# Gate products made early in place of plain gate units, in a hybrid retention and attention block

## The chip, the cores and the metric

The kernel runs on one core of one Trainium2 chip. The metric is the time of one execution in microseconds (us) on the device; the time shown for a kernel is the median of its runs. The engines are TensorE (PE, matmuls, with PEld for its weight loads), VectorE (DVE), ScalarE (ACT), GpSimd (POOL) and SyncE (SP, which issues most DMAs).

## What is computed

The input has 1024 tokens of 1024 channels; 16 meta tokens stand ahead of them. One input projection of the normalised tokens feeds everything else:

```python
u = rms_norm(h)
rq, rk, rv, rg, aq, ak, av, ag, gr, ga = split(u @ w_in)
o_r = groupnorm(retention_forward(rq, rk, rv) + retention_backward(rq, rk, rv))  # 4 heads, chunks of 128
y_r = (o_r * silu(rg)) @ w_rb
o_a = window_attention(aq, ak, av, sink)        # 8 heads, window of +-128, meta keys, sink
y_a = (o_a * silu(ag)) @ w_ab
out = (sigmoid(gr) * y_r + sigmoid(ga) * y_a) @ w_out
return h + rms_norm(out)
```

The gate columns of `w_in` are `rg`, `ag`, `gr` and `ga`: 4096 columns, 16 **units** of 256 columns.

## The kernel before

**Precision.** All matmuls that matter are made three times, for the float32 result: each operand is split into a high part (a copy in the matmul's format) and a low part (what the copy lost), and `mm3` (lines 69 to 71) adds high x high, low x high and high x low into the same PSUM bank. So one product of two 128-wide blocks is three matmuls, and every operand costs a copy (ACT or POOL) and a subtraction on DVE (`dve_lo`, line 77).

**Order of the work.** The code writes the program in one order; a scheduler then keeps that order as priorities and, on each engine, may take a later instruction when an earlier one is not ready. Tiles with the same tag share a fixed number of buffers, and `tc.issue_after(x)` puts what follows behind `x` on x's engine. The stages are:

1. Setup, and the first retention head's queries and keys.
2. Retention, heads 0 to 3 (`retention`). Each head has a forward pass over 9 chunks (`stage1` projects the values with `projT`, transposes the keys and makes scores; `stage2` makes the chunk's output `pa` and the state product `pkv`) and a backward pass over the chunks (`pb`, the normalisation, and the transposes `to` in `finish`). In the backward pass `fill(KT)` asks seven times for eight **fill steps**: pieces of an independent projection, each of three matmuls (one `mm3`), that PE does while the chain over the chunks waits. For heads 0 to 2 the filler is the next head's queries and keys (`gen_qk`). For head 3 it is the attention's keys, its first queries and one plain gate unit, `gen_gate(7)`. What the fills have not used, `drain()` does at the end of the head.
3. Attention, in four pairs of heads (`attention`), 8 blocks of 128 queries each. `FILL` says how many fill steps follow each block. For the last pair the filler is the second half of its queries (16 steps) and the plain gate units 6 and 5.
4. The phases z, r, a and o (`Phase` and `run`): the gate units, the two branch projections and the output projection. They use a seven-product form of the 2x2 block product: the weight unit is cut into 2x2 blocks A11 to A22, the input into B11 to B22, and seven products of 12 matmuls (4 x `mm3`, 512 columns) replace eight.

**A plain gate unit** (`gen_gate`, line 701) makes a gate unit in the ordinary way: 4 tiles of 8 x 3 matmuls, 96 in all, one fill step per `mm3`; DVE scales each tile, ACT takes the tanh and SP stores it. `N_GATE = 3` units are made so, and the other 13 run in phase z.

**A unit in z** goes through products 1, 5, 6, 2, 7, 3, 4, and two units are interleaved (u, u+1 at each product). `prepare` makes the left operand (sums of weight blocks into `st` tiles, then `split` into `lh` and `ll`), `LEAD = 6` jobs ahead: the step of product i prepares job i+5. `product` runs the 12 matmuls into a PSUM bank, `combine` adds the banks up:

- Products 1, 6, 7 and 4 add into one bank, X. After product 1 ACT copies it (`c1`), after 6 again (`u2`), after 7 again (`u3`); each copy has to be made before the next product adds to X.
- Product 2 goes to a bank Z, and `c1 + Z` is the output block (0, 0). Products 5 and 3 go to Y: `u3 + Y` after product 5 is block (1, 1), and `u2 + Y` after product 3 is block (0, 1). X after product 4 is block (1, 0).
- `z_post` scales a block (line 1006), takes SiLU or tanh, and for the first 8 units multiplies it by the branch output `v`, fetched from DRAM (`z_fetch`, tiles `g`).

When the last products of z have used the input blocks, `refill` loads the next phase's input and makes its blocks and differences: 28 splits (`split_b`, ACT copy at line 752 and `dve_lo`) and 16 subtractions (line 924). `refill` returns a table: at step -13 before the end of the phase do this, at -11 that. In between, `pre_split` makes the blocks of `w_out` for phase o at steps 30, 40, 50 and 60.

**Buffers named below.** `pj`: three PSUM banks for projections and fill steps. `wr`: two raw weight tiles; `wh` and `wl`: four split halves of a unit each. `g`: six tiles of 512 columns, shared by `v` and others.

Of the kernel before, what the change touches and what calls it, by code (L numbers as in the profile page):

```python
# [38 lines left out]
def block_kernel(ctx: ExitStack, tc: tile.TileContext, xT, x, w_in, w_rb, w_ab, w_out, vecs, dec, sink,  # L39
# [20 lines left out]
    mx_d = dram.tile([KT, P, SEQ], F32, tag="mx", name="mx_d")  # L60
    tg_d = dram.tile([2 * KT, P, SEQ], F32, tag="tg", name="tg_d")

    xs_d = {n: dram.tile([4, P, 512], F32, tag=f"xs{n}", name=f"xs{n}") for n in ("T1", "T2", "T3", "T4")}
    pre_d = {n: [dram.tile([P, 4, 512], F32, tag=f"pre{n}{s}", name=f"pre{n}{s}") for s in range(2)]
             for n in ("T1", "T2", "T3", "T4")}
# [363 lines left out]

    pend = []  # L430

    def retention(h, fill):
        q, kt = qk[h]
        qh, ql = [], []
        for i in range(2):
# [62 lines left out]
        def stage2(c):  # L498
            n, vh, vl, kd, s = st1.pop(c)
            if c > 0:  # L500
                fh, fl = state["fs"]
                pa = p3(f"pa{h}_{c}")
                mm3(pa[:, 0:256], s[0], s[1], vh, vl, True, True)
                mm3(pa[:, 256:512], qs(qh, c), qs(ql, c), fh, fl, True, True)
                o = op[c - 1]
                nc.scalar.activation(o, pa[:, 0:256], AF.Copy, scale=rcol[:, c:c + 1])
                nc.vector.scalar_tensor_tensor(o, pa[:, 256:512], qdf(h, c), o, op0=ALU.mult, op1=ALU.add)
            if kd:
                pk = p2(f"pkv{h}_{c}")
            if "f" in kd:  # L510
                a, b = kd["f"]
                mm3(pk[:, 0:256], a[0:n], b[0:n], vh[0:n], vl[0:n], True, True)
                new = rp.tile([P, 256], F32, tag="S", bufs=2, name=f"Sf{h}_{c}")
                if c == 0:
                    nc.vector.tensor_copy(new, pk[:, 0:256])
                else:
                    nc.vector.scalar_tensor_tensor(new, state["f"], cdf(h), pk[:, 0:256], op0=ALU.mult, op1=ALU.add)
                state["f"] = new
                state["fs"] = split_state(new, f"f{h}_{c}")
            if "b" in kd:  # L520
                a, b = kd["b"]
                mm3(pk[:, 256:512], a, b, vh, vl, True, True)
                nc.scalar.copy(kvb[c - 1], pk[:, 256:512])
# [174 lines left out]
            dve_lo(l, x[o], h)  # L698
            nc.sync.dma_start(pre_d[n][1][:, k], l.bitcast(F32))

    def gen_gate(u):

        w = load_w(w_in, U_GR + u)
        for a, b in HALVES:
            for e_ in range(2):
                t = yield from proj(w, P * e_, a, b, f"pgt{u}_{a}{e_}")
                o = ra.tile([P, 512], F32, tag="m1", bufs=2, name=f"gt{u}_{a}{e_}")
                nc.vector.tensor_tensor(o, t, rbc[:, a:b], ALU.mult)
                nc.scalar.activation(o, o, AF.Tanh, scale=0.5)
                nc.sync.dma_start(tg_d[2 * u + e_, :, a - NM:b - NM], o)  # L710
                yield

    with tc.issue_after(normed):
        evac_qk0(2)
        decay_table((0,))
        evac_qk0(3, 5)
    for h in range(NH):
        fill, drain = filler([*([gen_qk(h + 1)] if h < 3 else [gen_ak(0), gen_aq(0, 0), gen_gate(7)])])
        if h == 0:
            with tc.issue_after(normed):  # L720
                nc.vector.tensor_tensor(qd, rcol[:, 1:9].unsqueeze(1).to_broadcast([P, 2 * NH, NB]),
                                        dtab[:, 8:16].unsqueeze(2).to_broadcast([P, 2 * NH, NB]), ALU.mult)
        with tc.issue_after(rotated):
            retention(h, fill)
            drain()
    while pend:
        pend.pop(0)()
# [25 lines left out]
        dve_lo(l[:, k], src, h[:, k])  # L753

    class Phase:
        def __init__(self, nm, seq, load, post, fetch=None, apart=(), early=()):
            self.nm, self.seq, self.load, self.post, self.fetch = nm, seq, load, post, fetch
            self.apart, self.early = apart, early
            self.raw, self.s, self.ops, self.u = {}, {}, {}, {}
            self.cur = None  # L760

        def block(self, u, n):
# [16 lines left out]
        def prepare(self, u, p):  # L779
            if self.cur is not None and u // 2 != self.cur:  # L780
                self.raw = {}
            self.cur = u // 2
            g = nc.vector.tensor_tensor
            if self.fetch and p in POST and u not in self.early:
                self.fetch(u, *POST[p])
            if p in (1, 2, 4):
                self.split(u, p, self.block(u, PROD[p][0]))
            elif p == 7:
                t = lp.tile([P, 4, P], F32, tag="st", bufs=3, name=f"st{self.nm}{u}S3")
                g(t, self.block(u, "A11"), self.block(u, "A21"), sub)  # L790
                self.split(u, 7, t)
            elif p == 5:
                t = self.s[u] = lp.tile([P, 4, P], F32, tag="st", bufs=3, name=f"st{self.nm}{u}S")
                g(t, self.block(u, "A21"), self.block(u, "A22"), add)
                self.split(u, 5, t)
                g(t, t, self.block(u, "A11"), sub)
            elif p == 6:
                t = self.s[u]
                self.split(u, 6, t)
                if u in self.early:  # L800
# [43 lines left out]
        def combine(self, u, p, st):  # L844
# [42 lines left out]
            if "u3" in st and "Y" in st and "c22" not in st:  # L887
                st["c22"] = plus(new("c5") if (self.nm, u) == last[:2] else st["u3"], st["u3"], "Y")
                self.post(u, 1, 1, st["c22"])
                if early:  # L890
                    done("Y")

    LEAD = 6
# [18 lines left out]
    def refill(nm, src):  # L912
# [199 lines left out]
    def o_tail(o, a):  # L1112
# [4 lines left out]
        if a:  # L1117
# [6 lines left out]
    gates = [U_G + u for u in range(4)] + [U_AG + u for u in range(4)] + [U_GR + u for u in range(8)]  # L1124
# [175 lines left out]
    def fills(hp):  # L1300
# [127 lines left out]
```

## Time and profile before

| what | value |
|---|---|
| median of 3 runs | 1092.71 us (1090.38 to 1093.98) |
| the profiled execution | 1091.82 us |
| its span, first to last instruction | 1089.8 us |
| mean granted PE clock | 0.995 |
| data moved by DMA | 159.45 MB, 146 GB/s on average |

The profile is one execution. Its span leaves out what lies before the first and after the last instruction, here 2.0 us. "Busy" is the time in which an engine executes; matmuls overlap in the pipeline, so PE's busy time says only that it has work. In a row of stretches "(x904)" is the number of instructions that touch the stretch, and the last columns are the granted clock of PE as a share of full speed, the DMA engines' share and GB/s. In a row of groups, the numbers behind the bar are busy us, mean ns of one, and then the engine's idle time before them with who ended it. The names are those of the program's tiles: `bz` is a bank of phase z, `pgt` one of a plain gate unit.

### The profile page before, as it was taken

The numbers are of one execution on the slowest core, as the hardware profiler recorded it, in microseconds if no ns is written. First come the engines' busy times: TensorE is split into PE (matmuls) and PEld (weight loads), VectorE is DVE, ScalarE is ACT, GpSimd is POOL, SyncE is SP. The second block draws the span as 40 slices with busy tenths as digits, with TensorE's granted clock in tenths as the row PEclk, the third lists the DMA queues.
The fourth block names the chain that finished last, engine by engine and source line by source line (L and its number), as shares of the span: only waits on it lengthen the run. The fifth ranks groups of instructions, "written<-read, shape, count | busy, mean of one in ns | idle before, by whom it ended". The sixth has DMA issues, their size and how long they took to land.

```text
span 1089.8 us, 17221 instructions
## 1 busy us (share of the span) xinstructions
PE 1068.6 (98%) x5975; PEld 922.5 (85%) x5975; DVE 872.3 (80%) x1864; ACT 488.6 (45%) x1132; POOL 241.7 (22%) x346
## 2 busy tenths in 40 slices
PE   8999999999999999999999999999999999999996
PEld 7899999998989889988887888888888788787885
DVE  7897778877955988898667975888889899767765
ACT  7241432513314544545657643454456546433442
POOL 3235324233322544445220000000000000110032
PEclk9999999998999999999999999999999999999999
DMA  7121101111114871112115663779874755779463
GB/s 289 39 79 40 55 24 59 59 40 39 63 44 144 295 277 60 59 59 68 50 49 169 238 227 120 247 240 324 276 274 140 236 185 200 235 202 336 118 116 78
DMA packets 75799, 159.45 MB, mean 146 GB/s; under 512 B 8128, under 2 KB 19904, under 8 KB 74944
## 3 DMA queue, kind: packets, MB, share of 16 engines
q1 hardware_dynamic: 71824, 151.78, 40.4%
q0 software_dynamic: 3456, 6.29, 3.7%
q8 instruction: 47, 0.77, 0.3%
q10 hardware_dynamic: 432, 0.28, 0.1%
q14 instruction: 40, 0.33, 0.1%
HBM read 105.89 MB, written 52.43 MB: 145 GB/s over the span
## 4 chain that ended last, share of the span: by engine, by line
PE 86%; DVE 5%; issue 3%; DMA 3%; POOL 2%; ACT 1%; SPq 0%; POOLq 0%; DVEq 0%; ACTq 0%
PE bz L70 8%; PE bz L69 8%; PE bz L71 8%; PE pv L69 3%; PE pv L70 3%; PE pv L71 3%; PE br L70 2%; PE bo L70 2%; PE bo L69 2%; PE bo L71 2%; PE br L69 2%; PE br L71 2%; PE ba L70 2%; PE ba L71 2%; PE ba L69 2%
## 5 line engine op out<-in xcount | busy, mean ns | idle before, releaser
L1054 POOL DMA_DIRECT2D mx_d<-c1a x4 | 3.7, 918 | 391.5 <-DVE c1a L1045 391.5
L70 PE MATMUL bz<-big,llz 128*128 128x512 f32 x208 | 82.4, 396 | 0.0
L71 PE MATMUL bz<-big,lhz 128*128 128x512 f32 x208 | 81.9, 394 | 0.0
L69 PE MATMUL bz<-big,lhz 128*128 128x512 f32 x208 | 80.8, 394 | 0.0
L69 PE MATMUL pv<-wh,big 128*128 128x256 f32 x256 | 73.6, 288 | 1.3 <-DVE m_qk L162 1.3
L70 PE MATMUL pv<-wh,big 128*128 128x256 f32 x256 | 73.4, 287 | 0.0
L71 PE MATMUL pv<-wl,big 128*128 128x256 f32 x256 | 73.2, 286 | 0.0
L69 PE MATMUL bz<-T,lhz 128*128 128x512 f32 x156 | 61.6, 395 | 0.0
L70 PE MATMUL bz<-T,llz 128*128 128x512 f32 x156 | 61.5, 395 | 0.0
L71 PE MATMUL bz<-T,lhz 128*128 128x512 f32 x156 | 61.3, 394 | 0.0
L1205 ACT ACTIVATE p<-p,nm 128x400 f32<-128x400 f32 (+1 forms) x64 | 38.3, 598 | 44.0 <-DVE nm L1203 42.3
L77 DVE TENSOR_TENSOR wl<-wr,wh 128x1024 fp32r<-128x1024 f32 x34 | 47.4, 1398 | 4.6 <-POOL wh L74 4.4
L70 PE MATMUL paq<-big,wl 128*128 128x512 f32 x128 | 51.0, 398 | 0.0
L71 PE MATMUL paq<-big,wh 128*128 128x512 f32 x128 | 50.9, 398 | 0.0
L69 PE MATMUL paq<-big,wh 128*128 128x512 f32 x128 | 50.8, 397 | 0.1
L69 PEld LDWEIGHTS pv<-wh,big 128*128 128x128 f32 x256 | 48.9, 191 | 2.1 <-DVE m_qk L162 1.5
L1217 POOL TENSOR_SCALAR p<-p,den 128x400 f32<-128x400 f32 (+1 forms) x60 | 36.0, 610 | 63.9 <-DVE den L1211 52.0
L70 PEld LDWEIGHTS pv<-wh,big 128*128 128x128 f32 x256 | 48.9, 191 | 0.1
L71 PEld LDWEIGHTS pv<-wl,big 128*128 128x128 f32 x256 | 48.9, 191 | 0.0
L69 PEld LDWEIGHTS bz<-big,lhz 128*128 128x128 f32 x208 | 39.0, 188 | 9.4
L70 PEld LDWEIGHTS bz<-big,llz 128*128 128x128 f32 x208 | 39.1, 188 | 9.3 <-DVE llz L77 0.2
L71 PEld LDWEIGHTS bz<-big,lhz 128*128 128x128 f32 x208 | 39.2, 188 | 8.9
(616 smaller groups left out, 3641.0 us busy)
## 6 DMA issues: line engine op xcount, KB each, us to landing
wr<-in_w_in_dram SPq DMA_DIRECT2D x35, 512.0 KB, 3.6
wrz<-in_w_in_dram SPq DMA_DIRECT2D x28, 512.0 KB, 5.7
tg<-tg_d SPq DMA_DIRECT2D x32, 256.0 KB, 4.7
T<-preT SPq DMA_DIRECT2D x6, 1024.0 KB, 7.5
oTr_d<-ost SPq DMA_DIRECT2D x16, 256.0 KB, 2.1
xs<-in_xT_dram SPq DMA_DIRECT2D x16, 256.0 KB, 5.5
xsT<-xs SPq DMA_DIRECT2D x16, 256.0 KB, 5.7
oTa_d<-oa SPq DMA_DIRECT2D x16, 256.0 KB, 2.1
```

The source lines that it names most:

```text
L69: nc.tensor.matmul(o, ah, bh, start=first, stop=False, **kw)
L70: nc.tensor.matmul(o, al, bh, start=False, stop=False, **kw)
L71: return nc.tensor.matmul(o, ah, bl, start=False, stop=last, **kw).ins
L77: return nc.vector.tensor_tensor(o, i, hi.bitcast(F32), ALU.subtract).ins
L1054: nc.gpsimd.dma_start(d, to, accum_op=ALU.add)
L1205: nc.scalar.activation(p[:, 0:wid], p[:, 0:wid], AF.Exp, scale=-1.0, bias=nm_[:, e_:e_ + 1], accum_out=den[:, e_:e_ + 1])
L1217: nc.gpsimd.tensor_scalar(pt[e_][:, 0:wid], pt[e_][:, 0:wid], den[:, e_:e_ + 1], 1.0, op0=ALU.mult, op1=ALU.mult)
```

## The change

The plain gate units go (`N_GATE`, `gen_gate`), and all 16 gate units run in phase z. In their place 22 of the units' products are made early and kept in DRAM: product 2 for units 2 to 15, and product 3 also for units 8 to 15 (`PRE`). `gen_pre` loads the raw weights, makes the left operand (for a unit with two products with three DVE sums over 512 columns), splits it, runs 4 fill steps per product into a `pj` bank, copies the bank with ACT and stores it in `e_d`.

These fill steps stand at three places. In heads 1, 2 and 3 of the retention `between` asks, behind the forward state product of chunks 0 to 3, for one step (heads 1 and 2) or two (head 3). In the backward pass of head 3 a piece of 16 steps takes the place of the 32 steps of `gen_gate(7)`, between the keys and the queries. In the last attention pair the remaining 56 steps take the place of the 64 of `gen_gate(6)` and `gen_gate(5)`.

In z, `Phase` leaves the made products out of its sequence. Product 1's step fetches `e` for product 2 into a `g` tile and adds it to `c1`; product 6's step fetches `e` for product 3, and `u2` becomes the DVE sum of `e` and bank X where it was ACT's copy of X. The order of a unit is so 1, 5, 6, 7, 3, 4 for units 2 to 7 and 1, 5, 6, 7, 4 for units 8 to 15. The refill at the end of z has a table of its own.

```diff
-FILL = {**{h: (8, 8, 0, 8, 8, 8, 8, 0) for h in range(3)}, 3: (16, 16, 0, 16, 14, 10, 8, 0)}
-N_GATE = 3
+FILL = {**{h: (8, 8, 0, 8, 8, 8, 8, 0) for h in range(3)}, 3: (16, 16, 0, 14, 10, 8, 8, 0)}
+PRE = {u: (2, 3) if u > 7 else (2,) for u in range(2, 16)}
...
-                mm3(pk[:, 0:256], a[0:n], b[0:n], vh[0:n], vl[0:n], True, True)
+                forward = mm3(pk[:, 0:256], a[0:n], b[0:n], vh[0:n], vl[0:n], True, True)
+                if h and c < 4:
+                    with tc.issue_after(forward):
+                        between(h // 3 + 1)
...
+    def gen_pre(u):
+        g = nc.vector.tensor_tensor
+        n = P * len(PRE[u])
+        raw = [keep.tile([P, 4, 256], F32, tag="wr", bufs=2, name=f"we{u}_{j}") for j in range(len(PRE[u]))]
+        for j, t in enumerate(reversed(raw)):
+            nc.sync.dma_start(t[:, :, 0:n], w_in[gates[u], :, 4 - 4 * j:8 - 4 * j, 0:n])
+        t = raw[-1]
+        if n > P:
+            v = t[:, :, P:n]
+            g(v, raw[0][:, :, P:n], v, ALU.add)
+            g(v, v, raw[0][:, :, 0:P], ALU.subtract)
+            g(v, t[:, :, 0:P], v, ALU.subtract)
+        h = wp.tile([P, 4, 256], R, tag="wh", bufs=4, name=f"weh{u}")[:, :, 0:n]
+        l = wp.tile([P, 4, 256], R, tag="wl", bufs=4, name=f"wel{u}")[:, :, 0:n]
+        nc.scalar.copy(h, t[:, :, 0:n])
+        dve_lo(l, t[:, :, 0:n], h)
+        for p in PRE[u]:
+            b = pj(f"pe{u}_{p}")
+            m = slice(P * (p - 2), P * (p - 1))
+            c = slice(NM + 512 * (p - 2), NM + 512 * (p - 1))
+            for k in range(4):
+                mm3(b, h[:, k, m], l[:, k, m], xh[4 + k][:, c], xl[4 + k][:, c], k == 0, k == 3, True)
+                if k < 3:
+                    yield
+            o = ra.tile([P, 512], F32, tag=f"m{p - 1}", bufs=2, name=f"e{u}_{p}")
+            nc.scalar.copy(o, b)
+            nc.sync.dma_start(e_d[u, p], o)
+            yield
...
-        fill, drain = filler([*([gen_qk(h + 1)] if h < 3 else [gen_ak(0), gen_aq(0, 0), gen_gate(7)])])
+        fill, drain = filler([*([gen_qk(h + 1)] if h < 3 else [gen_ak(0), pieces(pre, 16), gen_aq(0, 0)])])
...
-            retention(h, fill)
+            retention(h, fill, filler([pieces(pre, (0, 4, 4, 8)[h])])[0])
...
             if p == 1:
                 copy("c1")
+                e = self.e.pop((u, 2), None)
+                if e is not None:
+                    nc.vector.tensor_tensor(st["c1"], st["c1"], e, add)
+                    self.post(u, 0, 0, st["c1"])
+            elif p == 6 and (u, 3) in self.e:
+                st["u2"] = new("u2")
+                plus(st["u2"], self.e.pop((u, 3)), "X")
+                self.post(u, 0, 1, plus(st["u2"], st["u2"], "Y"))
...
+        if nm == "z":
+            return {-16: [load(0, 0), load(0, 1)], -13: [load(1, 1)], -11: [plain("B22", 1, 1)],
+                    -9: [plain("B11", 0, 0)], -7: [t1, load(1, 0)], -5: [t2, t3], -4: [b21], -3: [plain("T3", 0, 1)],
+                    -1: [plain("T4", 0, 0)]}
...
-    steps = run([(Phase("z", sequence(16 - N_GATE, (1, 3, 2, 5, 6, 7, 4)), w_loader(w_in, gates), z_post, z_fetch,
-                        early=(0, 1)),
+    steps = run([(Phase("z", sequence(16, (1, 3, 2, 5, 6, 7, 4)), w_loader(w_in, gates), z_post, z_fetch,
+                        early=(0, 1), pre=PRE),
...
-            l += [gen_gate(6), gen_gate(5)]
+            l.append(pre)
```

Before, the table that z used was the common one: the splits of B11 at -13, `t1` at -11, `t2` and `t3` at -9, `b21` at -7, T3 at -5, B22 at -3 and T4 at -1.

More of the change, by code (lines that the diff above doesn't have):

```diff
@@ L430, in block_kernel, with retention @@
     pend = []
-    def retention(h, fill):
+    def retention(h, fill, between):
         q, kt = qk[h]
@@ L699, in pre_split, with pieces, all_pre @@
             nc.sync.dma_start(pre_d[n][1][:, k], l.bitcast(F32))
[L701 to L711, printed above, removed]
+    gates = [U_G + u for u in range(4)] + [U_AG + u for u in range(4)] + [U_GR + u for u in range(8)]
+    def gen_pre(u):
[26 more added lines that the diff above has]
+            yield
+    def pieces(gen, n):
+        for _ in range(n):
+            yield next(gen)
+    def all_pre():
+        for u in PRE:
+            yield from gen_pre(u)
+    pre = all_pre()
     with tc.issue_after(normed):
@@ L755, in block_kernel, with __init__ @@
     class Phase:
-        def __init__(self, nm, seq, load, post, fetch=None, apart=(), early=()):
-            self.nm, self.seq, self.load, self.post, self.fetch = nm, seq, load, post, fetch
+        def __init__(self, nm, seq, load, post, fetch=None, apart=(), early=(), pre={}):
+            self.nm, self.load, self.post, self.fetch, self.pre = nm, load, post, fetch, pre
+            self.seq = [(u, p) for u, p in seq if p not in pre.get(u, ())]
             self.apart, self.early = apart, early
-            self.raw, self.s, self.ops, self.u = {}, {}, {}, {}
+            self.raw, self.s, self.ops, self.u, self.e = {}, {}, {}, {}, {}
             self.cur = None
@@ L783, in prepare @@
             g = nc.vector.tensor_tensor
-            if self.fetch and p in POST and u not in self.early:
-                self.fetch(u, *POST[p])
+            made = {1: 2, 6: 3}.get(p)
+            if made not in self.pre.get(u, ()):
+                made = None
+            for q in (p, made):
+                if self.fetch and q in POST and u not in self.early:
+                    self.fetch(u, *POST[q])
+            if made:
+                self.e[u, made] = gtile(f"e{u}{made}")
+                nc.sync.dma_start(self.e[u, made], e_d[u, made])
             if p in (1, 2, 4):
@@ L799, in prepare @@
                 self.split(u, 6, t)
-                if u in self.early:
+                if u in self.early or 3 in self.pre.get(u, ()):
                     del self.s[u]
@@ L889, in combine @@
                 self.post(u, 1, 1, st["c22"])
-                if early:
+                if early or 3 in self.pre.get(u, ()):
                     done("Y")
```

2 lines of the change are left out of this document (1 added, 1 removed).

## The prediction

> **What bounds the kernel now.** I read the page first, then busy time by stretch, the groups of matmuls, and TensorE's (PE's) own waits.
>
> ```profile
> span 1089.8 us, 17221 instructions
> PE 1068.6 (98%) x5975; PEld 922.5 (85%) x5975; DVE 872.3 (80%) x1864; ACT 488.6 (45%) x1132; POOL 241.7 (22%) x346
> PE 86%; DVE 5%; issue 3%; DMA 3%; POOL 2%; ACT 1%; SPq 0%; POOLq 0%; DVEq 0%; ACTq 0%
> ```
>
> PE is busy for 98% of the span and carries 86% of the chain that ended last; VectorE (DVE) is second with 80%. The next rows are stretches of time, with busy us and instruction count of PE, PEld, DVE, ACT and POOL, then the granted PE clock and the DMA share. The first three are the borders between retention heads, then attention, its last head pair, the gate phase z, and the stretch in which z turns into the next phase, r.
>
> ```profile
> 118.00:126.00 8.00, 7.38 (x57) 6.50 (x56) 6.16 (x21) 3.77 (x12) 2.87 (x5) 1.00 0.14 45
> 186.00:194.00 8.00, 7.37 (x57) 6.50 (x56) 6.13 (x21) 3.77 (x12) 2.48 (x5) 1.00 0.19 63
> 254.00:268.00 14.00, 12.09 (x70) 10.79 (x69) 10.46 (x33) 4.97 (x17) 3.86 (x7) 0.76 0.12 39
> 340.00:500.00 160.00, 159.10 (x968) 141.25 (x967) 135.02 (x330) 77.72 (x228) 72.67 (x107) 1.00 0.41 142
> 500.00:588.00 88.00, 87.08 (x512) 76.34 (x510) 58.82 (x183) 53.42 (x156) 24.80 (x50) 1.00 0.20 70
> 590.00:798.00 208.00, 208.00 (x904) 168.47 (x903) 171.90 (x280) 106.33 (x190) 0.00 (x0) 1.00 0.71 244
> 798.00:858.00 60.00, 60.00 (x258) 48.14 (x257) 58.69 (x98) 38.16 (x69) 0.00 (x0) 1.00 0.60 201
> ```
>
> In z PE never rests. One matmul lasts 394 ns in the rows below, but they overlap: 904 touch the 208 us stretch, so one starts every (208 + 0.39) / 904 = 0.2305 us. That pitch, not the duration, is the price of a 512-column matmul. So a **product** (12 matmuls) is 2.77 us and a **fill step** (3 matmuls) 0.69 us. DVE is the engine to watch: from 798 to 858 it works 58.69 of 60 us on 98 operations, one every 0.60 us, and PE's 258 matmuls are 4 fewer than its pitch would give (60.39 / 0.2305 = 262), so 0.9 us is lost there already.
>
> **The change part by part.** First the PE work.
>
> ```profile
> L70 PE MATMUL bz<-big,llz 128*128 128x512 f32 x208 | 82.4, 396 | 0.0
> L69 PE MATMUL bz<-T,lhz 128*128 128x512 f32 x156 | 61.6, 395 | 0.0
> L71 PE MATMUL pgt<-big,wh 128*128 128x512 f32 x96 | 38.0, 396 | 0.0
> ```
>
> Each of these rows is one of three equal ones (lines 69, 70, 71). Today z has 3 x (208 + 156) = 1092 matmuls, which is 13 units x 7 products x 12, and the three plain gate units 3 x 96 = 288. Afterwards 16 units x 7 x 12 = 1344, of which 22 x 12 = 264 are made early and 1080 in z. 1380 becomes 1344: **36 fewer**, 36 x 0.2305 = **8.3 us**, if PE stays as full as it is. By place: the tail of head 3 of the retention loses 16 steps (32 gate steps become 16), its borders gain 16, the last attention pair loses 8, z loses one product.
>
> By the Trainium skill's page TensorE: Matmul & The Clock Gate, section Back-to-back issue gap, a sustained stream at N = 512 takes about 131 ns per matmul; the sum would then be an estimate of 4.7 us. The trace does not agree, at 0.2305 us over 904 matmuls, so that sum gets no chance of its own.
>
> **At the borders**, the new steps stand behind the forward product `pkv` of chunks 0 to 3. What PE waits for there:
>
> ```profile
> PE tr L466 <- ACT ost L560: 1.8, 3, 0.6
> PE to L555 <- DVE op L587: 1.0, 1, 1.0
> 258.23 0.41 PE L555 MATMUL to<-ident,op 128*128 128x128 f32 x2 [1.05 <-DVE op L587]
> 259.36 0.48 PE L466 MATMUL tr<-ident,kr 128*128 128x128 f32 x1 [0.61 <-ACT ost L560]
> 260.19 0.58 PE L69 MATMUL pkv<-vh,khf 16*128 16x256 f32 x1
> ```
>
> The three stretches leave 0.62 + 0.63 + 1.91 = 3.2 us of PE idle. 1.8 us of it are three transposes, one per border, and 1.0 us is `to`; the last rows show that both stand ahead of the first `pkv` (260.19), where the new steps may not go. So the steps can fill only 3.2 - 2.8 = **0.4 us**, and I take that; the ends are nothing and all 3.2. At the third border the clock is 0.76 over 14 us, which costs 14 x 0.24 = 3.4 us. The idle that precedes it stays, so I keep that cost; if it went, 3.4 us more would be won. The steps also hold one of three `pj` banks through chunks 0 to 3, which leaves `projT` two; I cost that at nothing, since PE has no other long wait there. If PE ran out of projections, one of them (24 matmuls of 256 columns) would be uncovered at each border: at half the 512-column pitch each, some 2.8 us.
>
> **In the attention** the fill shrinks from 80 steps to 72. Today 0.9 of 88 us are idle in the last pair, against 0.9 of 160 in the pairs before, which run on 8 steps a block; the new (14, 10, 8, 8) is nowhere below 8, so I cost the thinner cover at 0.5 us (ends: none, and all 8 steps, 5.5 us). The operands of the steps cost more than before:
>
> ```profile
> L77 DVE TENSOR_TENSOR wl<-wr,wh 128x1024 fp32r<-128x1024 f32 x2 | 2.4, 1220 | 0.0
> L708 DVE TENSOR_TENSOR gt<-pgt,rbc 128x512 f32<-128x512 f32 x8 | 5.5, 688 | 0.7 <-PE pgt L71 0.7
> wr<-in_w_in_dram SPq DMA_DIRECT2D x35, 512.0 KB, 3.6
> ```
>
> A unit with two products needs three sums of 512 columns (3 x 0.60) and one split of 1.22 us, 3.0 us; seven such units are 21 us, and 5.5 + 2.4 us go. DVE then has 58.8 + 13 = 72 of some 82 us, 88%; it has 84% (135 of 160) in the pairs before, where PE is full. One unit's chain is load 3.6, sums 1.8, split 1.2 and ACT's copy, which I take to be as long as the split: about 8 us for 5.5 us of PE work, but four split buffers let up to four units run ahead, and the stores of `e` are 256 KB on a DMA system 20% busy.
>
> **In z** units 2 to 7 lose product 2, units 8 to 15 products 2 and 3. A unit of 8 to 15 took 18 DVE operations in 7 products (7 splits, 4 sums, 3 adds, 4 scalings) and takes 16 in 5 (5, 3, 4, 4); the first eight units have 4 more, for the gating. With the refills, the sums for `w_out` and the blocks T2 to T4 I count 358 in z today and 390 afterwards, while its PE time falls from 91 to 90 products (249 us): 390 x 0.60 = 234 us, 94%. Where they bunch decides. In the last 11 products before r there are 35 operations of the products themselves and 44 of the refill of the input blocks (28 splits, 16 differences): 79 x 0.60 = 47.4 us against 11 x 2.77 = 30.4, so DVE ends 17 us behind. Operands are made 5 products ahead, 13.8 us; the excess is 3.2 us of PE waiting. The same count today, over the last 13 products, is 78 x 0.60 = 46.8 against 36.0: 10.8 us behind, inside the 13.8, as the loss of only 0.9 us bears out. Four operations (block B22, free since unit 7) can run earlier, 2.4 us. Between 0.8 and 3.2 I take **2.4 us**; the ends are nothing (PE takes other ready products) and 7 (DVE also waits for PE in strict order).
>
> A second price in z is the hand-over of the accumulator bank. In units 8 to 15 only one product stands between products 6 and 7 of a unit, and between 7 and 4, where there were three; and the reader after product 6 is now a DVE sum instead of an ACT copy.
>
> ```profile
> L850 ACT COPY u2z<-bz x13: 581/586/592, 618.7 to 823.1; 128x512 f32<-128x512 f32 x13
>   ACT u3z L850: 9.4, 6
>   ACT u2z L850: 6.2, 5
> ```
>
> Of 13 copies of each kind ACT stood waiting for the product 6 and 5 times; the others came later than at once. The slack is now 2.77 - 0.59 = 2.2 us. At the rate of the stretch before 798 (171.9 of 208 us) DVE is not behind by that much, so I take 0.5 us for all 16 hand-overs; the ends are nothing and 16 x 0.8.
>
> The 22 loads and 22 stores of `e` (11.5 MB) and the two weight loads of 512 KB for each of three more units lie beside a DMA share of 0.71 in z; the loads are issued 5 products (13.8 us) ahead and like ones land in 5.7:
>
> ```profile
> wrz<-in_w_in_dram SPq DMA_DIRECT2D x28, 512.0 KB, 5.7
> ```
>
> I cost them at nothing; without that lead the SP queue would hold them up by some 5 us once.
>
> **Sum:** -8.3 - 0.4 + 0.5 + 2.4 + 0.5 = **-5.3 us**. The profiled execution took 1091.82 us (its span and 2.0 us around it), 0.9 below the median 1092.71; it becomes 1086.5, the median 1087.4.
>
> **The rivals.**
>
> *Full gain, 1081 to 1084.* PE takes other products while DVE catches up, as today's 0.9 us speaks for, and at best the third border keeps its clock: 1092.7 - 8.7 = 1084.0, less 3.4 = 1080.6. Against it: 17 us behind is more than the lead.
>
> *The clock drops where z becomes r, about 1095.* DVE's 7 us in strict order leave PE idle in long pieces, and half clock follows for 3.4 us: 1092.7 - 8.7 + 1.0 + 7 + 3.4 = 1095.4. For it: at the third border 1.05 and 0.61 us of idle were enough. The same page, section HAM oscillation, puts the point at gaps over about 3.4 us; the border does not agree with it as a lower limit.
>
> *The bank hand-over is the bound; slower.* If DVE's answer to products 6 and 7 comes 3.0 us after them, 0.8 over the slack, 16 hand-overs cost 12.8: 1092.7 - 8.7 + 0.5 + 2.4 + 12.8 = 1099.7. It decides from a mean lag of about 2.2 + 5.8 / 16 = 2.6 us. For it: DVE at 94% of z; against it: the rate before 798.
>
> *The steps are not there when wanted; no change, 1092.* The change then does not do what it says. The two raw buffers serialise the chain of 8 us a unit; if each of seven units comes 0.7 us late, 4.9 us go and 1092.3 is left. Against: the four buffers that run ahead.
>
> **How the numbers follow.** Chances: forecast (1084 to 1089) 0.48, full gain 0.20, clock drop 0.12, bank hand-over 0.10, late steps 0.10. 0.3% (3.3 us, 1089.4 to 1096.0) is about what a measurement of this kernel can tell from no change. Faster: 0.45 of the forecast and the full gain, 0.65. Same: 0.03, the late steps and 0.07 of the clock drop, 0.20. Slower: the hand-over and 0.05, 0.15. The range 1081 to 1095.5 leaves out the hand-over, 0.03 of the clock drop and 0.04 below.
>
> **What would show it.** 1080 matmuls `bz` and 264 new ones, pitch 0.23: the first term. PE waits before `pkv` at the borders as long as now: 0.4 us right. DVE without idle for longer than 60 us around the end of z, and fewer than 262 matmuls per 60 us of it: the 2.4. PE waits before `bz` spread over units 8 to 15 would mean hand-overs, and a clock under 1.00 at a new place the third rival. Idle before the new matmuls between 500 and 580 would mean late steps.

## The result and the profile after

| | before | after |
|---|---|---|
| median of 6 runs | 1092.04 us | 1122.66 us |
| lowest to highest | 1090.38 to 1093.98 | 1121.26 to 1123.89 |
| the profiled execution, its span | 1091.82, 1089.8 | 1123.0, 1121.2 |
| mean granted PE clock | 0.995 | 0.979 |

The kernel became slower: the ratio is 1.0279, with a 95% interval of 1.0265 to 1.0294. The prediction said 1087.4, with a range up to 1095.5. From the page of the changed kernel (span, busy time, granted clock in 40 slices of 28 us, chain):

```profile
span 1121.2 us, 17340 instructions
PE 1077.6 (96%) x5939; PEld 923.3 (82%) x5939; DVE 909.6 (81%) x1916; ACT 511.9 (46%) x1168; POOL 238.0 (21%) x340
PEclk9999799898999999999999999999999999999998
PE 57%; DVE 10%; DMA 6%; ACT 1%; issue 1%; POOL 0%; SPq 0%; DVEq 0%; POOLq 0%; ACTq 0%
```

PE has the 36 matmuls less (5975 to 5939) and yet more busy time, since a matmul at half clock is longer. The clock has holes in the fifth, eighth and tenth slice, the first at 112 to 140 us, long before z; half clock took 1121.2 x 0.021 = 23.5 us of full speed, before 1089.8 x 0.005 = 5.4. PE's share of the chain fell from 86% to 57%. With the 8.3 us that the 36 matmuls should have saved, PE lost 31.5 + 8.3 = **39.8 us** by waiting and by the clock. Where, the trace tells by the start of each stage's first matmul (us; the prediction's names):

| start of | before | after | later by | matmuls alone | lost in the stage ahead of it |
|---|---|---|---|---|---|
| attention, `pav` | 330.56 | 353.01 | 22.4 | 0 | 22.4, retention |
| z, `bz` | 589.01 | 617.47 | 28.5 | -5.5 | 11.5, attention |
| a, `ba` | 915.23 | 945.82 | 30.6 | -8.3 | 4.9, z and r |
| the end | 1089.75 | 1121.23 | 31.5 | -8.3 | 0.9, a and o |

The last row is the end of the last instruction; where attention overlaps with what stands ahead of it, the start of `pav` is a rough border. The fifth column is what the change does to the number of matmuls up to there, at 0.2305 us each: 24 fewer ahead of z (22 products in place of 24), 12 fewer in z. The rows below are stretches with the columns of the prediction: the borders of the first heads, a stretch of the third attention pair, z, and its end.

```profile
95.00:119.00 24.00, 17.57 (x95) 13.55 (x93) 21.98 (x61) 5.74 (x17) 13.35 (x18) 0.77 0.19 66
119.00:126.00 7.00, 7.00 (x32) 6.45 (x32) 1.68 (x5) 0.67 (x2) 0.48 (x1) 0.56 0.12 40
186.00:197.00 11.00, 7.69 (x48) 5.87 (x47) 10.19 (x30) 3.63 (x13) 4.67 (x7) 0.84 0.24 85
500.00:520.00 20.00, 18.53 (x81) 15.30 (x82) 19.17 (x38) 4.47 (x15) 7.90 (x10) 0.83 0.13 41
619.00:826.00 207.00, 206.95 (x897) 167.26 (x896) 187.24 (x309) 113.49 (x203) 0.00 (x0) 1.00 0.82 282
826.00:886.00 60.00, 57.17 (x245) 45.41 (x243) 57.80 (x96) 35.79 (x64) 0.00 (x0) 1.00 0.72 243
```

The same stretches before:

```profile
95.00:119.00 24.00, 24.00 (x191) 23.05 (x190) 20.92 (x55) 5.18 (x17) 12.09 (x17) 1.00 0.21 67
186.00:197.00 11.00, 10.37 (x82) 9.50 (x81) 8.10 (x27) 5.06 (x17) 3.03 (x6) 1.00 0.14 46
500.00:520.00 20.00, 20.00 (x117) 17.67 (x116) 17.30 (x46) 11.59 (x35) 9.43 (x15) 1.00 0.24 80
```

From 95 to 119 us PE now does 95 matmuls where it did 191, and it is not new work that displaced them: the first new step comes at 119.98 us. What is missing shows in the groups of the projections `pv` between 95 and 119 us (count; duration min, median, max in ns; first and last start), after:

```profile
L71 PE MATMUL pv<-wh,big x8: 276/281/283, 101.0 to 103.5; 128*128 128x256 f32 x8
```

and before, as L69:

```profile
L69 PE MATMUL pv<-wh,big x44: 274/281/364, 100.7 to 118.9; 128*128 128x256 f32 x44
```

A projection of a chunk has 8 of them: one is made in that time now, five and a half were. PE's order of time, after, at the first border (start, duration, engine, line, tile; in brackets PE's idle time and who ended it):

```profile
104.09 0.28 PE L73 MATMUL pv<-wl,big 128*128 128x256 f32 x1
105.58 0.36 PE L71 MATMUL pb<-Shb,qh 128*128 128x256 f32 x1 [1.22 <-DVE rs L591]
...
107.69 0.35 PE L71 MATMUL pb<-Shb,qh 128*128 128x256 f32 x1 [1.29 <-DVE op L585]
...
110.08 0.55 PE L71 MATMUL pb<-Shb,qh 128*128 128x256 f32 x1 [1.75 <-DVE op L585]
...
119.98 0.80 PE L71 MATMUL pe<-big,weh 128*128 128x512 f32 x1
...
121.42 0.41 PE L71 MATMUL pv<-wh,big 128*128 128x256 f32 x1
121.64 0.41 PE L72 MATMUL pv<-wh,big 128*128 128x256 f32 x1
```

Before, at the same border:

```profile
120.07 0.28 PE L69 MATMUL pb<-Shb,qh 128*128 128x256 f32 x1
...
120.78 0.27 PE L70 MATMUL pv<-wh,big 128*128 128x256 f32 x1
120.89 0.28 PE L71 MATMUL pv<-wl,big 128*128 128x256 f32 x1
121.01 0.38 PE L555 MATMUL to<-ident,op 128*128 128x128 f32 x2
```

Before, PE filled the backward chain (`pb`) with the next head's projections (`pv`), up to 120.89 us. After, `pv` ends at 104.09 us and comes back at 121.42, right behind the first new step `pe` at 119.98. Between the two, PE only follows the chain. The idle pieces shown are 1.2 to 1.8 us long. After the first two the granted clock is at half, from 108.2 us on, and the matmuls of 256 columns start 0.22 us apart where it was 0.11; the third piece falls into the half clock already.

The Trainium skill's page TensorE: Matmul & The Clock Gate, section A second HAM failure mode: psum-queue depth-cycling, says that short idle pieces between groups of matmuls can also bring the clock down. The trace agrees: the two pieces ahead of the half clock are 1.22 and 1.29 us long.

### The profile page after: what moved, and what is told of

Its sections match the earlier page's. It is cut to its first block, busy times and chain, and to the rows that moved or that the text cites. A ratio compares the mean times of both kernels' runs of the same rounds, so it can differ in the third digit from the quotient of the medians.

```text
span 1121.2 us, 17340 instructions
## 1 busy us (share of the span) xinstructions
PE 1077.6 (96%) x5939; PEld 923.3 (82%) x5939; DVE 909.6 (81%) x1916; ACT 511.9 (46%) x1168; POOL 238.0 (21%) x340
## 4 chain that ended last, share of the span: by engine, by line
PE 57%; DVE 10%; DMA 6%; ACT 1%; issue 1%; POOL 0%; SPq 0%; DVEq 0%; POOLq 0%; ACTq 0%
PE bz L71 5%; PE bz L72 5%; PE bz L73 5%; PE bo L72 2%; PE bo L71 2%; PE bo L73 2%; PE paq L71 2%; PE paq L72 2%; PE paq L73 2%; DMA we<-in_w_in_dram 2%; PE ba L72 2%; PE br L71 2%; PE br L72 2%; PE ba L73 2%; PE br L73 2%; PE ba L71 2%
## 5 line engine op out<-in xcount | busy, mean ns | idle before, releaser
L71 PE MATMUL pv<-wh,big 128*128 128x256 f32 x256 | 75.1, 293 | 1.2 <-DVE m_qk L164 1.2
L72 PE MATMUL bz<-T,llz 128*128 128x512 f32 x192 | 75.7, 394 | 0.0
L71 PE MATMUL bz<-T,lhz 128*128 128x512 f32 x192 | 75.6, 396 | 0.1
L73 PE MATMUL bz<-T,lhz 128*128 128x512 f32 x192 | 75.6, 395 | 0.0
L72 PE MATMUL pv<-wh,big 128*128 128x256 f32 x256 | 74.6, 291 | 0.0
L72 PE MATMUL bz<-big,llz 128*128 128x512 f32 x168 | 66.6, 396 | 0.0
L73 PE MATMUL bz<-big,lhz 128*128 128x512 f32 x168 | 66.2, 394 | 0.0
L71 PE MATMUL bz<-big,lhz 128*128 128x512 f32 x168 | 65.3, 394 | 0.0
L71 PEld LDWEIGHTS pv<-wh,big 128*128 128x128 f32 x256 | 50.9, 199 | 2.2 <-DVE m_qk L164 1.5
L71 PE MATMUL paq<-big,wh 128*128 128x512 f32 x128 | 52.4, 409 | 0.0
L73 PE MATMUL paq<-big,wh 128*128 128x512 f32 x128 | 51.9, 405 | 0.0
L72 PEld LDWEIGHTS pv<-wh,big 128*128 128x128 f32 x256 | 50.6, 198 | 0.8
L566 ACT ACTIVATE ost<-to,rnw 128x128 f32<-128x128 f32 x64 | 20.0, 364 | 63.0 <-PE to L561 56.0
L1259 DVE CUSTOM_DVE_ANT_0 p<-ps,mask,nsink 128x400 f32<-128x400 f32 (+1 forms) x64 | 36.4, 596 | 11.1 <-PE pt L1290 9.3
L71 PEld LDWEIGHTS bz<-T,lhz 128*128 128x128 f32 x192 | 36.1, 188 | 9.2 <-DVE u2z L898 0.5
L73 PEld LDWEIGHTS bz<-T,lhz 128*128 128x128 f32 x192 | 36.1, 188 | 8.5
```

Of the source, the lines that this page charges most:

```text
L71: nc.tensor.matmul(o, ah, bh, start=first, stop=False, **kw)
L72: nc.tensor.matmul(o, al, bh, start=False, stop=False, **kw)
L73: return nc.tensor.matmul(o, ah, bl, start=False, stop=last, **kw).ins
L566: nc.scalar.activation(ost[0][:, e_, w0:w0 + P], to[:, P * e_:P * e_ + P], AF.Copy, scale=rnw[:, 2 * h + e_:2 * h + e_ + 1])
L1259: nc.vector.tensor_tensor_reduce(p[:, 0:wid], s[:, 0:wid], mask[:, mo:mo + wid], -SCALE, nsink[:, hd:hd + 1], ALU.add, ALU.min, nm_[:, e_: ...
```

## The experiments

All times are medians, ratios are to the kernel before, with the 95% interval. Where each stage starts later (or earlier, -) than in the kernel before, in us, from the trace:

| kernel | `pav` | `bz` | `ba` | end |
|---|---|---|---|---|
| changed kernel | 22.4 | 28.5 | 30.6 | 31.5 |
| no steps at the borders | -2.5 | 7.2 | 9.7 | 9.6 |
| steps at the borders, not pinned | -5.8 | 1.6 | 10.1 | 10.2 |
| kernel before, a bank held | 27.6 | 18.8 | 20.8 | 21.5 |
| no steps at the borders, without sums | -3.3 | -6.8 | 1.5 | 1.5 |
| no steps at the borders, without refill subtractions | -2.0 | 5.4 | 2.7 | 3.6 |
| no steps at the borders, without both | -1.9 | -5.8 | -4.4 | -3.7 |
| product 2 only | -13.7 | -18.5 | 4.2 | 5.1 |
| product 2 only, all in the attention | -25.1 | -16.8 | 7.5 | 8.0 |

**The borders: 21 us, and it is the pinned bank.** The theory: the tile of the new step takes one of the three `pj` banks, the step may not run before the forward product, and so the projections behind it in program order get no bank early. The rival was that the steps themselves, or their loads and operands, cost the time. First kernel, no steps at the borders, their 16 go to head 3's backward pieces:

```diff
-                if h and c < 4:
-                    with tc.issue_after(forward):
-                        between(h // 3 + 1)
...
-... pieces(pre, 16), gen_aq(0, 0)])])
+... pieces(pre, 32), gen_aq(0, 0)])])
...
```

> The changed kernel without the steps at the borders of the retention's heads: the four products of units 2 to 5 follow in the backward piece of head 3, which grows from 16 steps to 32. The number of products and matmuls is unchanged. Theory P (pinned bank): a product at a border takes its projection bank in program order but may not begin before the first forward product, so the next head's projections behind it can no longer run in the backward pass; the idle time and the half clock that follows are the retention's loss. The retention then costs what it did before, some 20 us less than in the changed kernel: 1100 to 1104 us. Theory O (operands): the splits and loads for early products disturb the retention wherever they are made, most of the loss moves along: 1113 us or more.

1101.56 us, 1.0096 (1.0075 to 1.0118): 21 us of the 31 go by the medians, 20 by the ratios. The next kernel keeps the steps but drops the pin:

```diff
-                    with tc.issue_after(forward):
-                        between(h // 3 + 1)
+                    between(h // 3 + 1)
```

> The changed kernel with the border steps at the same place of the program, but not put behind the forward product, so that PE may take them as soon as their operands are there. Theory P: the bank no longer stands reserved and idle, the projections follow, and most of the 20 us come back: 1101 to 1108 us, with no half clock at the first two borders. Theory O: loads, splits and copies are the same, so the time stays at 1118 to 1124 us.

1106.52 us, 1.0143 (1.0125 to 1.0161): 16 us go by the medians, 5 fewer than without the steps. The profiled execution is the fastest of its four, 1101.75 us, and so not typical of that median. In it the attention starts even earlier than in the kernel before, so nothing is lost at the borders; it loses more in z (11.3 us, by the table and the 2.8 us of the matmuls). And the opposite: the kernel before, with one `pj` bank pinned over chunks 0 to 3 of heads 1 to 3 (two in turn in head 3). Nothing is loaded for it, its 12 matmuls are 2.8 us of work, and an ACT copy ends it:

```diff
+                if h and c < 4:
+                    with tc.issue_after(forward):
+                        if c == 0 or h == 3 and c == 2:
+                            state["hold"] = pj(f"hold{h}_{c}")
+                        nc.tensor.matmul(state["hold"], xh[0][:, NM:NM + P], xh[0][:, NM:NM + 512], start=True,
+                                         stop=True)
...
```

> The kernel before with a projection bank held at the borders of heads 1 to 3 and nothing else: one matmul behind the forward product of each of chunks 0 to 3, into a projection bank that ACT copies out at the end (two banks in turn in head 3); the copy is not used further. No weights are loaded or split for it, 12 matmuls are 2.8 us. Theory P: the retention loses about what the changed kernel loses there, 13 to 22 us, so 1108 to 1117 us, with half clock at the first two borders. Theory O: only the matmuls and copies cost, 1094 to 1097 us.

1113.73 us, 1.0207 (1.0192 to 1.0223). The stretch 95 to 119 us, without the pin:

```profile
95.00:119.00 24.00, 24.00 (x181) 22.56 (x180) 20.48 (x50) 6.08 (x18) 12.74 (x16) 1.00 0.28 88
```

and in the kernel before with the bank held:

```profile
95.00:119.00 24.00, 17.52 (x94) 13.59 (x93) 22.23 (x60) 5.37 (x17) 14.02 (x19) 0.80 0.22 70
```

The steps without the pin leave PE full (24.00 us, 181 matmuls, clock 1.00); the pin without the rest takes PE to 94 matmuls, as in the changed kernel (95). By its ratio, holding the bank costs 22.6 us, less the 2.8 of its own matmuls 19.8, about what the first kernel won back. So the rival falls as the cause of the bulk; up to the 5 us that the median without the pin lies above the first kernel may still be due to the steps. Bank and pin are not separated: no kernel pins a step that holds no bank. Why 8.8 of the 27.6 us by which `pav` is late with the bank held are made up by `bz` stays open.

**The attention: the sums of three blocks.** The first kernel still reached z 7.2 us later than before, though it has 24 matmuls less ahead of z (5.5 us): 12.7 more than the matmuls give. Next the three VectorE sums of units 8 to 15 were left out, so that their product 3 is made from an operand that isn't summed.

```diff
-        if n > P:
-            v = t[:, :, P:n]
-            g(v, raw[0][:, :, P:n], v, ALU.add)
-            g(v, v, raw[0][:, :, 0:P], ALU.subtract)
-            g(v, t[:, :, 0:P], v, ALU.subtract)
```

> The first kernel of this list without the three DVE sums that make the left operand of product 3 of units 8 to 15 (the output then lacks that part of the gates). It is compared with the first kernel. Theory D (DVE): in the attention the changed kernel loses some 12 us because the sums, 1.8 us of DVE per unit, are pulled into the third head pair, where DVE is nearly full; without them 6 to 10 us come back, 1091 to 1097 us. Theory F (fill): the loss is that fill steps are used up early and 72 are too few; then it stays within 3 us of the first kernel.

1096.28 us, 1.0039 (1.0029 to 1.0050). z starts 6.8 us earlier than before: the whole loss of the attention is gone, and 1.3 us more. The stretch in which the attention's second pair gives way to the third, with the sums:

```profile
470.00:490.00 20.00, 17.07 (x85) 14.14 (x84) 18.81 (x46) 9.21 (x30) 9.38 (x12) 0.83 0.26 93
```

without them:

```profile
470.00:490.00 20.00, 20.00 (x113) 17.06 (x113) 19.16 (x47) 8.63 (x29) 9.99 (x13) 1.00 0.15 53
```

DVE is at 94 to 96% in both, but with other work. With the sums, nine of them start between 454 and 488 us, though the first early product in the attention starts at 505.8 us and PE never idles ahead of one. PE waits instead for the row maxima of the softmax (`nm`) and the rotated queries (`m_aq`), which DVE makes too:

```profile
PE ps L71 <- DVE nm L1255: 2.5, 4, 1.0
PE paq L71 <- DVE m_aq L164: 1.6, 1, 1.6
```

Neither is among the nine longest waits without the sums, and in the stretch PE does 85 matmuls with them and 113 without. That it is the order of DVE's work, and not its amount, is a reading of the trace: this kernel takes away both. The end, though, is only 8.1 us earlier than with the sums, where z's start is 13.9 earlier: the rest is lost again in z.

**Work moved to GpSimd.** To take load off DVE, the 16 subtractions of the refill at the end of z, or the sums, or both, went to GpSimd (`nc.gpsimd` in place of `nc.vector`) in the first kernel, and the 16 subtractions also in the kernel before.

> The kernel without border steps (1101.6 us), with the 16 subtractions of the refill at the end of z made by POOL, which is idle there, in place of DVE. Theory B (backlog): DVE ends z some 17 us behind, more than the lead of 13.8 us, and PE waits some 5 us there; 16 operations of 0.60 us less are 9.6 us, which brings it below the lead: 1096 to 1099 us, with PE waits of under 1.5 us between 820 and 880. Theory H (hand-over of the bank): the waits are those of a bank that is read late and not of operands that are made late; then 1100 to 1103 us.

> The kernel without border steps (1101.6 us), with the three sums of product 3's left operand for units 8 to 15 made by POOL in place of DVE. Theory D (DVE's time): the attention loses because 1.8 us of DVE per unit fall where DVE is full, so taking them off DVE gives back what leaving them out gave: 1090 to 1096 us. Rival L (latency): the attention loses because an operand is ready late, by its chain of load, sums, copy and split; POOL's sums are no shorter, so nothing comes back, 1100 to 1106 us.

> Both together: no border steps, the sums of product 3 and the refill's subtractions at the end of z on POOL. If theories B and D hold, the losses in the attention and at the end of z are gone and the 36 matmuls fewer show: 1085 to 1091 us, faster than both kernels. If H and L hold, 1099 us or more.

> The kernel before with the refill's 16 subtractions at the end of z on POOL. Theory B: there DVE was 11 us behind, inside the lead, and PE lost 0.9 us, so at most that comes back: 1090.5 to 1092 us. If DVE at the end of z costs more than it shows in PE's gaps, 1087 to 1089 us.

They took 1107.13 us (1.0143, 1.0124 to 1.0163), 1108.04 (1.0153, 1.0127 to 1.0180), 1114.83 (1.0201, 1.0177 to 1.0224) and, from the kernel before, 1101.99 (1.0102, 1.0085 to 1.0118). All are slower than the kernel they start from, and outside every range that was expected but that of the third, whose 1099 us or more was open upwards. GpSimd and DVE in the last of them, in order of time:

```profile
810.45 20.40 POOL L924 TENSOR_TENSOR z<-z,z 128x512 f32<-128x512 f32 x12 [232.80 <-DMA tg<-tg_d]
...
833.78 1.26 POOL L924 TENSOR_TENSOR z<-z,z 128x512 f32<-128x512 f32 x1 [0.62 <-DVE T L77]
```

```profile
814.29 1.78 DVE L77 TENSOR_TENSOR llz<-wrz,lhz 128x512 fp32r<-128x512 f32 x1
816.00 1.78 DVE L77 TENSOR_TENSOR llz<-stz10S,lhz 128x512 fp32r<-128x512 f32 x1
...
833.62 0.68 DVE L853 TENSOR_TENSOR c1z<-c1z,bz 128x512 f32<-128x512 f32 x1
```

While GpSimd subtracts (12 in 20.40 us, 1.70 each), DVE's own subtractions start 1.70 us apart and last 1.78 us where they last 0.68; they go in step with GpSimd's. With the sums on GpSimd the same shows in the attention: a `den<-den,es` (L1262) beside a sum lasts 1.28 us where another lasts 0.15. So these four do not test whether DVE has too much to do: they made it slower. What they do show is that the kernel before has little room there: with 16 subtractions of up to 1.70 us each on GpSimd and DVE slowed beside them it is 11 us slower.

**The end of z: the refill.** So the work was left out in place of moved. This kernel leaves the 16 subtractions at the end of z out of the first one, and r multiplies by the blocks as they are:

```diff
         def minus(o, a, b):
-            nc.vector.tensor_tensor(x[*o], x[*a], x[*b], sub)
+            if nm != "z":
+                nc.vector.tensor_tensor(x[*o], x[*a], x[*b], sub)
```

> This is the kernel of e1 without the 16 VectorE subtractions that make r's operands at the end of z (it leaves them out; r multiplies by the blocks as they are). Reference points: e1 1101.6 us (first z product 7.2 us later than before, end 9.7 later), before 1091. Theory B (VectorE's backlog at the end of z starves the first products of r): 16 x 0.65 = 10.4 us of VectorE's work goes in the last dozen products, so the br waits of some 5 us go and the time falls to 1096 to 1098. Theory H (the hand-over of the banks between the pairs of z, which doesn't hang on the refill, costs the 5 us): within 1.5 us of e1.

1095.37 us, 1.0026 (1.0014 to 1.0039). 60 us around the end of z, with the subtractions:

```profile
812.00:872.00 60.00, 56.65 (x237) 43.81 (x236) 58.60 (x97) 35.24 (x63) 0.00 (x0) 1.00 0.69 231
```

without them:

```profile
812.00:872.00 60.00, 60.00 (x260) 48.56 (x259) 52.94 (x87) 36.91 (x67) 0.00 (x0) 1.00 0.72 242
```

DVE goes from 98% to 88%, PE from 237 matmuls to 260 without a gap. From z's first product to a's, this kernel takes 2.7 us less than before, just what the 12 matmuls fewer in z are worth (2.8), where with the subtractions it was 2.5 more: the backlog costs 5.2 us. With the subtractions PE's waits between 826 and 900 us are these, and without them there is none:

```profile
PE br L71 <- ACT lhr L809: 1.7, 3, 0.7
PE br L72 <- DVE llr L79: 1.5, 2, 1.4
```

They are for r's weight operands and not for the blocks that the subtractions make, so it is DVE's backlog and not the refill's own chain that PE waits for. Theory H, a loss at each hand-over of a bank, falls for this kernel.

**Both left out.** No steps at the borders, no sums, no subtractions at the end of z:

> The kernel of e4 (no steps at the borders, the sums of three blocks left out) without the 16 VectorE subtractions at the end of z, so it leaves out both parts of the computation. If VectorE's work is all that stands between the 36 fewer matmuls and the time, this is 8 us faster than before: 1082 to 1086. If hand-overs of banks in z take part of it, as the two short half clocks in z of e4 hint (2.2 and 3.1 us of stalls, 3.4 us of half clock), 1087 to 1092.

1089.13 us, 0.9970 (0.9956 to 0.9985), the only one faster than before, but not in the 1082 to 1086 that DVE's work alone would have given: it lies in the range with the hand-overs. The spans differ by 3.8 us, so 4.5 of the 8.3 us are still missing, though nothing is lost ahead of z (-5.8 us for 5.5 us of matmuls). From z to a 4.2 us are lost, and 2.7 of them are one wait:

```profile
PE bz L71 <- ACT u3z L886: 2.7, 1, 2.7
```

ScalarE's and the stretch's rows say why the copy `u3z` was late:

```profile
714.35 0.62 ACT L698 CAST wT11h<-w 128x512 fp32r<-128x512 f32 x1 [2.01 <-DVE w L696]
716.71 0.62 ACT L698 CAST wT31h<-w 128x512 fp32r<-128x512 f32 x1 [1.74 <-DVE w L696]
717.23 0.58 ACT L886 COPY u3z<-bz 128x512 f32<-128x512 f32 x1
```

```profile
700.00:730.00 30.00, 27.34 (x118) 21.87 (x117) 26.78 (x45) 14.01 (x25) 0.00 (x0) 1.00 0.99 349
```

The copy stands behind two casts for phase o's operands. They wait for DVE, and DVE waits for loads of `w_out` (1.56 and 1.06 us, ended by the DMA) while the DMA engines are 99% busy; before, from 700 to 730 us, they were at 77%. A full DMA system alone is not the cause: before, from 730 to 760 us, it was at 97% and PE had no gap. Which transfers held the loads up wasn't tried. The rest is in smaller pieces, 1.5 us in z and 0.7 behind it, whose cause wasn't sought.

**Two versions meant to be better.** Product 2 has no sums. So: `PRE = {u: (2,) for u in range(2, 16)}`, no steps at the borders, 16 steps in head 3 and 40 in the attention, product 3 back in z, and the refill spread over z's last 12 products.

> Only product 2 of units 2 to 15 is made ahead (14 products, 16 steps of them in the last head's backward pieces, 40 in the last pair of the attention), nothing at the borders, no sums of three blocks; product 3 goes back to z, and z's last pair has 12 products over which the refill is spread. The matmuls are the 36 fewer of the changed kernel. If the losses are those of the pinned bank, of the sums in the attention and of the refill squeezed into 10 products, all three are gone and the 8.3 us of the matmuls show: 1083 to 1087. Theory H (each z pair without product 2 hands its banks over with a loss, since products 1, 5, 6 and 7, 3, 4 of a pair follow each other more closely in time than the copies of their sums): 14 units lose some 0.5 us each, 1089 to 1094. If the attention runs out of fill, with 120 matmuls in place of 192, the first z product would come about as early as before and not 22 us earlier: 1100 or more.

1096.09 us, 1.0033 (1.0021 to 1.0045), between the ranges that were expected. From z to a 3.2 us are lost (22.6 later for 84 matmuls more, 19.4). But z starts 18.5 us earlier where 120 matmuls less ahead of it are 27.7: 9.2 us are lost in the attention, since up to `pav` nothing is (-13.7 for 11.1 us of matmuls). Then all 56 steps in the attention:

```diff
-... [gen_ak(0), pieces(pre, 16), gen_aq(0, 0)])])
+... [gen_ak(0), gen_aq(0, 0)])])
...
-FILL = ... 3: (16, 8, 0, 8, 8, 8, 8, 0)}
+FILL = ... 3: (16, 16, 0, 14, 10, 8, 8, 0)}
```

> The kernel of e10 with its 14 products 2 all in the last pair of the attention (56 steps, 168 matmuls, over the fill places that the changed kernel has) and none in the last head. Theory C (in e10 the attention lost some 9 us because 120 matmuls are too thin a cover where before had 192, and the last head needs no cover: pav came 13.7 us earlier in e10 for 11.1 us of matmuls taken out): pav about 25 us before that of before, first z product 25 to 28 us earlier than before (e10 18.5), end 1084 to 1089. Rival D (VectorE and ScalarE in the attention are the bound, whatever PE has to fill in): the first z product stays 17 to 20 us earlier, end 1093 to 1097.

1100.81 us, 1.0090 (1.0071 to 1.0109), above both ranges. Theory C fell: the attention starts 25.1 us earlier, as it said, but z only 16.8, 10.9 short of the matmuls. Two stretches of the attention in this kernel:

```profile
360.00:420.00 60.00, 56.87 (x353) 49.32 (x352) 54.89 (x133) 27.96 (x82) 31.97 (x44) 1.00 0.57 207
420.00:480.00 60.00, 57.09 (x319) 48.47 (x317) 47.74 (x141) 32.47 (x104) 23.49 (x42) 0.97 0.11 36
```

and in the kernel before:

```profile
360.00:420.00 60.00, 59.19 (x307) 49.68 (x306) 54.98 (x119) 25.67 (x73) 31.04 (x39) 1.00 0.69 246
420.00:480.00 60.00, 59.91 (x394) 54.81 (x394) 51.78 (x146) 32.09 (x103) 26.89 (x48) 1.00 0.17 56
```

PE idles in the first two pairs already, where nothing was changed but the time at which they start, and DVE is no fuller than before there. PE's longest wait in these 120 us is again for the row maxima `nm`, 3.0 us. That speaks for the softmax chain as the limit, which PE's fill only covers; it isn't shown, and which link of the chain sets the pace wasn't tried. No version that computes everything beat the kernel before.

## Why the prediction was wrong

In the prediction's own form, by the first table: -8.3 + 22.4 (borders) + 11.5 (attention) + 4.9 (z) + 0.9 (a and o) = 31.4 us, where it had -8.3 - 0.4 + 0.5 + 2.9 = -5.3.

- **36 fewer matmuls, -8.3.** Right in number and, by PE's pitch in z, in price, but no kernel here shows more than 3.8 us of it in its span. In order, the groups of the early products, and those of z (two of six rows; the six add up to 1080):

```profile
L71 PE MATMUL pe<-big,weh x88: 388/396/795, 120.0 to 612.4; 128*128 128x512 f32 x88
L71 PE MATMUL bz<-T,lhz x192: 390/393/503, 642.1 to 875.3; 128*128 128x512 f32 x192
L71 PE MATMUL bz<-big,lhz x168: 387/395/475, 617.5 to 853.8; 128*128 128x512 f32 x168
```

- **The borders, -0.4: the step that failed.** The prediction named the right object, "The steps also hold one of three `pj` banks through chunks 0 to 3", and wrote "I cost that at nothing, since PE has no other long wait there." It took the absence of waits as a sign of slack. PE had no wait there because the projections pulled ahead through those banks filled it. The bound, one projection a border (2.8 us), counted the bank from chunk 0 on; the bank is taken in program order, so it is missing all through the tail of the head before. The true size is 22.4 us by the trace, 20 to 21 by the kernel without the steps, half clock included. At the third border the prediction counted with the half clock that was there; it did not ask whether the other two could fall to it.
- **The attention, +0.5 (up to 5.5).** Wrong: 11.5 us. The count of DVE's work (88%) was an average over the pair; the sums run when their buffers and loads are there, ahead of the softmax. The prediction feared that the operands come too late; they came too early. PE idles before none of the early products' matmuls in the last pair, so the rival of the late steps falls.
- **The end of z, +2.4 (up to 7).** The mechanism was right, the size off: 4.9 us in the changed kernel, 5.2 by experiment. The 60 us around it have 245 matmuls, under the 262 that the prediction set as the mark. The clock is 1.00 there, so the rival of a clock that drops where z becomes r did not come; it dropped at the borders and in the attention.
- **The hand-over of the banks, +0.5.** In the changed kernel at most that: in the row 619 to 826 PE has 897 matmuls, where the pitch of 0.2305 us gives 899.7, so 0.6 us are lost. The slower rival's 12.8 us are not there: it named the right direction with the wrong mechanism.
- **The loads and stores of `e`, nothing.** True in the changed kernel, where PE shows one wait of 0.05 us in z before its end. In the kernel that reaches z earlier 2.7 us go to late loads of `w_out`; whether those of `e` delay them isn't shown.

## What to carry to other kernels

Where PE is full, ask first what fills it: work that a scheduler pulls ahead through shared buffers shows no wait in a trace, and it is the first thing to go when a buffer is pinned. So cost a pinned tile by what its buffers let run early, from the point in program order at which it is allocated. And cost early work on a second engine by what it can overtake there, not by that engine's average.

## What was not expected of the hardware

DVE's subtractions with both inputs in SBUF went from 0.68 to 1.78 us while GpSimd subtracted, while the addition of a PSUM bank stayed at 0.68 us: the one at 833.62 us lies in part beside the subtraction at 833.78, and one at 837.92 us lies wholly beside one of 1.65 us that starts at 837.48. The Trainium skill's page SBUF — State Buffer, section Who interferes with whom, has the rule: a DVE instruction with two SBUF inputs contends with a GpSimd instruction that reads SBUF, and one with at most one SBUF input, outside the two-port modes, does not. The trace agrees with both halves; the rule would have warned against moving such work to GpSimd here.

The clock fell to half at the first border, at about 108 us, after idle pieces of 1.22 and 1.29 us within 3.4 us, with matmuls between them.
